# Two matmuls of 256 columns for one of 512 in block 2's first feed-forward layer, and norm sums in halves of 128 columns

## Chip, cores and metric

One core of one Trainium2 chip runs the whole program in one launch. The metric is device time in microseconds (us), the median over several runs; smaller is better.

## What is computed

Two transformer-like blocks for 256 tokens of width 1024. The first has a gated linear attention branch, a spatial gating branch and a retrieval of single-neuron experts. The second takes the tokens `x` and a context `ctx` of 256 rows and begins with the same feed-forward layer for both:

```
def rmsnorm_2(x, w):
    xf = x.astype(jnp.float32)
    y = xf * lax.rsqrt(jnp.mean(xf * xf, axis=-1, keepdims=True) + EPS)
    return (y * w.astype(jnp.float32)).astype(x.dtype)

def swiglu(h, w13, w2):
    a, b = jnp.split(h @ w13, 2, axis=-1)
    return (jax.nn.silu(a) * b) @ w2
...
        x = x + 0.5 * g1x * swiglu(modulate(rmsnorm_2(x, norm_ffn1[l]), sh1x, sc1x), w13_ffn1[l], w2_ffn1[l])
        ctx = ctx + 0.5 * g1c * swiglu(modulate(rmsnorm_2(ctx, norm_ffn1[l]), sh1c, sc1c), w13_ffn1[l], w2_ffn1[l])
```

After it come retention, a Fourier branch, a second feed-forward layer for the tokens alone, and a last norm. The width `D_MODEL` is 1024, `D_FF` is 2816.

## The kernel before

Activations lie with the features on the 128 partitions and the 256 tokens (T) along the free dimension, in 8 chunks (KD). A weight unit is 128 by 1024 floats (512 KB). SyncE loads it into `raw`; ScalarE casts it to `whi` (fp32r, line 112) and VectorE makes the rest `wlo` (line 113). An activation is kept as two parts likewise. A product is three matmuls, `mm3` (lines 248 to 251): whi with the high part, whi with the low part, wlo with the high part. Each matmul has its own weight load (PEld in the profile), of 128 columns.

The order of the work is a hand-made list of items that `Emit.run` (line 91) walks through; each weight unit is an item, and three units are split ahead. Small steps are put behind later units with `em.later`.

`ffn` (line 468) is a feed-forward layer. There are 22 steps j. `up` (line 539) makes the two halves of the first product for step j, two units each of 24 matmuls, and `down` (line 557) adds the second product of step j - 2, one unit of 24 matmuls of 256 columns. In block 2's first layer the steps from `early` = 2 on have tokens and context side by side in the tiles `nxh` and `nxl` (128 by 8 by 512 floats), so that one matmul streams 512 columns into one PSUM bank. Steps 0 and 1 take a copy of the tokens that is not yet normalized, `y` (258 columns), and the context, `nhi` and `nlo` (256 columns), apart. Behind the steps the context's own second product follows (`down_c`, line 1623), in matmuls of 256 columns.

The norms' sums of squares over the features are made on TensorE: `ones_sum` (line 259) multiplies a 128 by 128 matrix of ones with the squares, plain fp32. Eight places call it: `norm1`, `norm2`, `ctx_norm` (twice), `sum_x` in `rest_c` (line 1463; it runs in step 6 of the first layer, between its two halves), `x_sums`, `rest_f2`, and `f2_done` (line 1961), the end of the program. Seven give it one tile of 512 columns, the last gives it four, `qs`, as ScalarE makes them. The trace lists each fp32 matmul as two.

`rest_c` also has a sum of its own, line 1450: eight fp32 matmuls of 256 columns, ahead of the context's product of step 1.

`GAP` (line 39) is a table of paddings in floats, put ahead of tiles; `open_d` puts GAP["nx"] ahead of `nxh`.

Of the kernel before, what the change touches and what calls it, by code (L numbers as in the profile page):

```python
# [20 lines left out]
P = 128  # L21
T = 256
# [13 lines left out]

TS = 320

GAP = {"n": 48, "ya": 40, "y": 48, "mc": 0, "nx": 32, "q": 48, "v": 16, "sc": 48, "y01": 0, "fo": 40, "f2": 32, "mh": 48}

NE = 7

# [160 lines left out]
def body(ctx, tc, I, out):  # L203
    nc = tc.nc
    act, dve, pe, pool = nc.scalar, nc.vector, nc.tensor, nc.gpsimd
# [10 lines left out]
    def bankA():  # L216
        return psA.tile([P, 512], F32, name="acc", tag="acc")

    def bankB():
        return psB.tile([P, 512], F32, name="wk", tag="wk")  # L220
# [27 lines left out]
    def mm3(o, whi, wlo, xhi, xlo, start, stop):  # L248
        pe.matmul(o, whi, xhi, start=start, stop=False)  # L249
        pe.matmul(o, whi, xlo, start=False, stop=False)  # L250
        pe.matmul(o, wlo, xhi, start=False, stop=stop)  # L251
# [6 lines left out]

    def ones_sum(qs, bank=bankB):
        ps = bank()  # L260
        for j, q in enumerate(qs):
            for a in range(2):
                pe.matmul(ps[:, :T], ones, q[:, a * T:a * T + T], start=j + a == 0, stop=a == 1 and j == len(qs) - 1)
        return ps

    def qsum(qs):
# [102 lines left out]
    def gap(pl, name):  # L369
        if GAP[name]:  # L370
            pl.tile([P, GAP[name]], F32, name="gap" + name, tag="gap" + name)

# [8 lines left out]
    def apair():  # L381
        return [npool.tile([P, T], F32R, name=n, tag=n, bufs=2) for n in ("ah", "al")]

    def split(src, hi, lo):
        act.copy(hi, src)  # L385
        dve.tensor_tensor(out=lo, in0=src, in1=hi, op=ALU.subtract)  # L386
# [6 lines left out]
    def chunks(o, hi, lo, x, width, order=range(KD)):  # L393

        xh, xl = x
        for k in order:
            sl = slice(k * P, k * P + P)
            mm3(o, hi[:, sl], lo[:, sl], xh[:, k, :width], xl[:, k, :width], k == order[0], k == order[-1])
# [54 lines left out]
    def gate_y(pa_, pb_, wk):  # L453

        ca, cb = shifted(pa_, wk), shifted(pb_, wk)
        s = wk.tile([P, T], F32, name="xs", tag="xs", bufs=2)
        u = wk.tile([P, T], F32, name="nn", tag="nn", bufs=3)
        dve.tensor_tensor(out=s, in0=pa_[:, :T], in1=E_["r"], op=ALU.mult)
        dve.tensor_tensor(out=u, in0=pb_[:, :T], in1=E_["r"], op=ALU.mult)

        def silu():
            act.activation(out=s, in_=s, func=AF.Silu, bias=ca)

        def prod():
            dve.scalar_tensor_tensor(out=s, in0=u, scalar=cb[:, 0:1], in1=s, op0=ALU.add, op1=ALU.mult)
        return s, silu, prod

    def ffn(w13, w2, y, nx, wk, done, rest, early, ctx=None, mc=None):

        acc = Acc()
        hold = {}
        items = []

        def gate_c(j):
            ps = hold.pop(("c", j))
            s = wk().tile([P, T], F32, name="cs", tag="cs", bufs=1)
            act.activation(out=s, in_=ps[:, 0:T], func=AF.Silu)  # L480
            dve.tensor_tensor(out=s, in0=s, in1=ps[:, T:], op=ALU.mult)
            em.later(lambda: split(s, *mc(j)))

        def gate(j):
            pa_, pb_ = hold.pop(("ps", j, 0)), hold.pop(("ps", j, 1))
            both = ctx is not None and j >= early
            if j < early:
                s, silu, prod = gate_y(pa_, pb_, wk())
            else:
                w = 2 * T if both else T  # L490
                f = wk().tile([P, w], F32, name="s2", tag="s2", bufs=2)
                s = f[:, :T]

                def silu():
                    act.activation(out=f, in_=pa_[:, :w], func=AF.Silu)

                def prod():
                    dve.tensor_tensor(out=f, in0=f, in1=pb_[:, :w], op=ALU.mult)

            def low():  # L500
                hold["m", j] = apair()
                split(s, *hold["m", j])
                if both:
                    split(f[:, T:], *mc(j))

            if j < 2:
                silu()
                if ctx is not None:
                    prod()
                else:  # L510
                    em.later(prod, 1)
                em.later(low, 0 if ctx is not None else 1)
                return

            hold["low", j] = low
            if ctx is not None or j == NFF - 1:
                silu()
                prod()
            else:
                em.later(silu)  # L520
                em.later(prod, 1)

        def bank(j, half):
            if ctx is None:
                return bankA() if j == 2 else bankB()
            return bankA() if j == half == 1 else bankB()

        def up0(sp):
            if ctx is not None:
                c = hold["c", 0] = bankB()  # L530
                for n, (hi, lo) in enumerate(sp):
                    chunks(c[:, n * T:n * T + T], hi, lo, ctx(), T)
            ps = [bank(0, n) for n in range(2)]
            hold["ps", 0, 0], hold["ps", 0, 1] = ps
            mm3s([p[:, :T + 2] for p in ps], sp, *y(), T + 2)
            if ctx is not None:
                em.later(lambda: gate_c(0))

        def up(j, half):
            def fn(hi, lo):  # L540
                ps = hold["ps", j, half] = bank(j, half)
                if j >= early:
                    w = T if ctx is None else 2 * T
                    chunks(ps[:, :w], hi, lo, nx(), w)
                else:
                    if ctx is not None:
                        if half == 1:
                            hold["c", j] = bankA()
                        chunks(hold["c", j][:, half * T:half * T + T], hi, lo, ctx(), T)
                    chunks(ps[:, :T + 2], hi, lo, y(), T + 2)  # L550
                if half == 0:
                    if j < early and ctx is not None:
                        em.later(lambda: gate_c(j))
                    em.later(lambda: gate(j))
            return fn

        def down(j):
            def fn(hi, lo):
                mh, ml = hold.pop(("m", j))
                acc.step(hi, lo, mh, ml, j == 0, j == NFF - 1)  # L560
                f = hold.pop(("low", j + 2), None)
                if f is not None and ctx is None and j + 2 == NFF - 1:
                    em.soon.append(f)
                elif f is not None:
                    em.later(f, 0 if ctx is not None else 1)
                if j == NFF - 1:
                    done(acc)
            return fn

        def begun():  # L570
            rest()
            em.later(lambda: gate(0), 0 if ctx is not None else 1)

        items += [("w", [w13[0], w13[NFF]], up0), ("e", None, begun)]
        for j in range(1, NFF):
            items.append(("w", w13[NFF + j], up(j, 1)))
            items.append(("w", w13[j], up(j, 0)))
            if ctx is not None and j > 1:
                items.append(("w", w2[j - 2], down(j - 2)))
            elif 2 < j < NFF - 1:  # L580
                for n in (0, 1) if j == 3 else (j - 2,):
                    items.append(("w", w2[n], down(n)))

        for n in range(NFF - 2 if ctx is not None else NFF - 3, NFF):
            items.append(("w", w2[n], down(n)))
        return items
# [10 lines left out]
    ones = const.tile([P, P], F32, name="ones")  # L597
# [102 lines left out]
    ya = (pa.tile([P, 4, T], F32R, name="yah"), pa.tile([P, 4, T], F32R, name="yal"))  # L700
# [247 lines left out]
    mh = pa.tile([P, KD, T], F32R, name="mh")  # L948
# [357 lines left out]
    sc = 0  # L1306
    for j in range(NQ, 16):
        n = min(j - 1, sc + (3 if j > NQ else 0))
        items += [score(i) for i in range(sc, n)]
        sc = n  # L1310
# [188 lines left out]
    n = len(ADA_A)  # L1499
# [82 lines left out]
    def mc(j):  # L1582

        t, c = (B["n"], j - 2) if j in MCN else (M["mc"], j if j < 2 else j - KD)
        return [m[:, c, :] for m in t]
# [418 lines left out]
    for h in range(4):  # L2004
        g = [gunit(h, j) for j in range(4)]
        v = tm(I["wv"][4 * h:4 * h + 4], [XN, XC], ev_v, bankA)
        k, q = qk(h, 1), qk(h, 0)
# [116 lines left out]
```

## Time and profile before

| what | value |
| --- | --- |
| median of 3 runs | 1959.22 us (1956.07 to 1961.68) |
| the profiled execution's own time | 1956.7 us |
| its span | 1955.0 us |
| TensorE busy, matmuls | 1938.9 us (99%) |
| TensorE busy, weight loads | 1860.3 us (95%) |
| VectorE busy | 1391.5 us (71%) |
| ScalarE busy | 1018.0 us (52%) |

A matmul's record lasts longer than the distance to the next one, since they overlap: 277 ns for 256 columns, with the next start some 113 to 118 ns later. So the cost of a matmul is read from starts, or from how many fall into a stretch, and not from its duration. The granted clock in the page's slices is full throughout.

### The profile page before, as it was taken

How to read it: one execution, taken by the hardware profiler on the slowest of the kernel's cores; microseconds unless marked ns; L12 is line 12 of the kernel's file. 1: busy time of each engine (PE TensorE's matmuls, PEld its weight loads, DVE VectorE, ACT ScalarE, POOL GpSimd, SP SyncE). 2: the span in 40 equal slices, each digit the busy share in tenths (PEclk: the TensorE clock that was granted, in tenths of full speed). 3: DMA queues.
4: the chain of work that ended last, by engine and by line, in shares of the span. 5: the costliest groups of instructions: out<-in, count | busy, mean ns of one | idle time of the engine just before them, and what ended most of it. 6: DMA issues, size and time to landing. Idle time of an engine off the chain costs nothing.

```text
span 1955.0 us, 37794 instructions
## 1 busy us (share of the span) xinstructions
PE 1938.9 (99%) x15348; PEld 1860.3 (95%) x15348; DVE 1391.5 (71%) x2282; ACT 1018.0 (52%) x1510; POOL 152.8 (8%) x296
## 2 busy tenths in 40 slices
PE   9999999999999999999999999999999999999998
PEld 8899999999999999999988888899989999999998
DVE  7667788987776776798866776578754556578655
ACT  6554655467776555555563333245744455446444
POOL 0000011111112001111000000010000000000000
PEclk9999999999999999999999999999999999999999
DMA  7655577766667778897755566677643334455663
GB/s 245 199 165 186 184 227 231 253 219 198 202 202 238 251 243 271 289 295 254 216 198 171 185 198 217 199 243 268 203 124 97 116 110 133 149 176 172 195 195 128
DMA packets 110094, 393.18 MB, mean 201 GB/s; under 512 B 14103, under 2 KB 14487, under 8 KB 109536
## 3 DMA queue, kind: packets, MB, share of 16 engines
q1 hardware_dynamic: 85968, 310.55, 50.5%
q0 software_dynamic: 22944, 77.52, 12.0%
q8 instruction: 120, 1.97, 0.4%
q10 hardware_dynamic: 1008, 2.70, 0.4%
q14 instruction: 54, 0.44, 0.1%
HBM read 371.84 MB, written 18.87 MB: 200 GB/s over the span
## 4 chain that ended last, share of the span: by engine, by line
PE 93%; DMA 2%; DVE 2%; ACT 1%; issue 0%; SPq 0%; ACTq 0%; DVEq 0%; POOLq 0%
PE wk L249 18%; PE wk L251 17%; PE wk L250 17%; PE acc L250 10%; PE acc L249 10%; PE acc L251 10%; PE acc L425 2%; PE acc L427 2%; PE acc L426 2%; DVE wlo L113 1%; PE acc L1255 1%; PE acc L1256 1%; DMA raw<-w_dram 1%; DMA raw<-f2a_dram 1%; ACT whi L112 1%; DMA raw<-f13a_dram 1%
## 5 line engine op out<-in xcount | busy, mean ns | idle before, releaser
L113 DVE TENSOR_TENSOR wlo<-raw,whi 128x1024 fp32r<-128x1024 f32 x587 | 716.4, 1223 | 464.2 <-ACT whi L112 460.5
L112 ACT CAST whi<-raw 128x1024 fp32r<-128x1024 f32 x587 | 615.9, 1050 | 650.9 <-PE wk L250 276.4
L249 PE MATMUL wk<-nhi,whi 128*128 128x256 f32 x1648 | 465.1, 282 | 1.3 <-ACT whi L112 1.3
L251 PE MATMUL wk<-nhi,wlo 128*128 128x256 f32 x1648 | 457.1, 277 | 0.8 <-DVE wlo L113 0.8
L250 PE MATMUL wk<-nlo,whi 128*128 128x256 f32 x1648 | 457.2, 277 | 0.0
L250 PE MATMUL acc<-al,whi 128*128 128x256 f32 x1376 | 382.9, 278 | 0.1
L249 PE MATMUL acc<-ah,whi 128*128 128x256 f32 x1376 | 382.6, 278 | 0.0
L251 PE MATMUL acc<-ah,wlo 128*128 128x256 f32 x1376 | 382.4, 278 | 0.0
L249 PEld LDWEIGHTS wk<-nhi,whi 128*128 128x128 f32 x1648 | 309.9, 188 | 2.4 <-ACT whi L112 1.5
L251 PEld LDWEIGHTS wk<-nhi,wlo 128*128 128x128 f32 x1648 | 310.0, 188 | 1.0 <-DVE wlo L113 1.0
L250 PEld LDWEIGHTS wk<-nlo,whi 128*128 128x128 f32 x1648 | 310.2, 188 | 0.5 <-issue 0.5
L250 PEld LDWEIGHTS acc<-al,whi 128*128 128x128 f32 x1376 | 259.4, 189 | 1.4 <-DVE al L386 0.5
L249 PEld LDWEIGHTS acc<-ah,whi 128*128 128x128 f32 x1376 | 258.5, 188 | 0.8
L251 PEld LDWEIGHTS acc<-ah,wlo 128*128 128x128 f32 x1376 | 259.2, 188 | 0.0
L249 PE MATMUL wk<-nxh,whi 128*128 128x512 f32 (+1 forms) x544 | 188.4, 346 | 0.0
L251 PE MATMUL wk<-nxh,wlo 128*128 128x512 f32 (+1 forms) x544 | 187.5, 345 | 0.0
L250 PE MATMUL wk<-nxl,whi 128*128 128x512 f32 (+1 forms) x544 | 186.5, 343 | 0.0
L385 ACT CAST ah<-early 128x256 fp32r<-128x256 f32 x128 | 52.1, 407 | 150.3 <-PE acc L251 147.0
L251 PEld LDWEIGHTS wk<-nxh,wlo 128*128 128x128 f32 x544 | 102.1, 188 | 14.1
L250 PEld LDWEIGHTS wk<-nxl,whi 128*128 128x128 f32 x544 | 102.2, 188 | 12.4
L249 PEld LDWEIGHTS wk<-nxh,whi 128*128 128x128 f32 x544 | 102.4, 188 | 11.5
L1269 POOL DMA_DIRECT2D uD<-act x128 | 69.1, 540 | 367.6 <-ACT act L1268 308.0
(526 smaller groups left out, 3345.2 us busy)
## 6 DMA issues: line engine op xcount, KB each, us to landing
raw<-pu_dram SPq DMA_DIRECT2D x128, 512.0 KB, 4.0
raw<-pv_dram SPq DMA_DIRECT2D x128, 512.0 KB, 4.4
row<-ada_dram POOLq DMA_DIRECT2D x59, 512.0 KB, 4.6
raw<-f13a_dram SPq DMA_DIRECT2D x44, 512.0 KB, 3.5
raw<-f2a_dram SPq DMA_DIRECT2D x44, 512.0 KB, 4.5
raw<-f13b_dram SPq DMA_DIRECT2D x44, 512.0 KB, 3.5
raw<-w_dram SPq DMA_DIRECT2D x41, 512.0 KB, 4.3
uD<-act POOLq DMA_DIRECT2D x128, 128.0 KB, 4.0
```

The costliest lines, as they stand in the source:

```text
L112: nc.scalar.copy(hi, r)
L113: nc.vector.tensor_tensor(out=lo, in0=r, in1=hi, op=ALU.subtract)
L249: pe.matmul(o, whi, xhi, start=start, stop=False)
L250: pe.matmul(o, whi, xlo, start=False, stop=False)
L251: pe.matmul(o, wlo, xhi, start=False, stop=stop)
L385: act.copy(hi, src)
L425: pe.matmul(o, xh[:, k, ts], hi[:, sl], start=k == 0, stop=False)
L426: pe.matmul(o, xh[:, k, ts], lo[:, sl], start=False, stop=False)
L427: pe.matmul(o, xl[:, k, ts], hi[:, sl], start=False, stop=k == KD - 1)
L1255: pe.matmul(o, p2[:, k, :, t], ph[:, k, :, t], start=True, stop=False)
L1256: pe.matmul(o, p2[:, k, :, t], p1[:, k, :, t], start=False, stop=True)
L1269: pool.dma_start(out=uD[:, b, :], in_=u)
```

## The change

`up` of block 2's first layer makes one product over the 256 token columns and then one over the 256 context columns, with the same weights, in the two halves of the same PSUM bank. `ones_sum` makes the first 128 columns of its sum over all its inputs, and then the other 128. GAP["nx"] becomes 0, which moves `nxh`, `nxl` and the tiles behind them in their pool by 128 bytes a partition.

```
-GAP = {"n": 48, "ya": 40, "y": 48, "mc": 0, "nx": 32, "q": 48, "v": 16, "sc": 48, "y01": 0, "fo": 40, "f2": 32, "mh": 48}
+GAP = {"n": 48, "ya": 40, "y": 48, "mc": 0, "nx": 0, "q": 48, "v": 16, "sc": 48, "y01": 0, "fo": 40, "f2": 32, "mh": 48}
...
     def ones_sum(qs, bank=bankB):
         ps = bank()
-        for j, q in enumerate(qs):
-            for a in range(2):
-                pe.matmul(ps[:, :T], ones, q[:, a * T:a * T + T], start=j + a == 0, stop=a == 1 and j == len(qs) - 1)
+        for c in range(0, T, P):
+            for j, q in enumerate(qs):
+                for a in range(0, 2 * T, T):
+                    pe.matmul(ps[:, c:c + P], ones, q[:, a + c:a + c + P], start=j + a == 0,
+                              stop=a == T and j == len(qs) - 1)
         return ps
...
                 if j >= early:
-                    w = T if ctx is None else 2 * T
-                    chunks(ps[:, :w], hi, lo, nx(), w)
+                    for c in range(1 if ctx is None else 2):
+                        ts = slice(c * T, c * T + T)
+                        chunks(ps[:, ts], hi, lo, [m[:, :, ts] for m in nx()], T)
```

TensorE's order where `sum_x` stands between two units of the first layer; the names are out<-moving,weights with buffer numbers, `wk` is a PSUM bank, `scr` holds the squares. Before:

```order
L250 MATMUL wk_13926<-nxl_13081,whi_13842 128x512
L251 MATMUL wk_13926<-nxh_13080,wlo_13843 128x512
L263 MATMUL wk_13957<-scr_13185,ones_98 128x256 x2
L249 MATMUL wk_13966<-nxh_13080,whi_13877 128x512
L250 MATMUL wk_13966<-nxl_13081,whi_13877 128x512
```

and now, at the same place:

```order
L250 MATMUL wk_14123<-nxl_13086,whi_14015 128x256
L251 MATMUL wk_14123<-nxh_13085,wlo_14016 128x256
L264 MATMUL wk_14178<-scr_13190,ones_98 128x128 x4
L249 MATMUL wk_14189<-nxh_13085,whi_14074 128x256
L250 MATMUL wk_14189<-nxl_13086,whi_14074 128x256
```

The sum stands between the same two units; the matmuls on both sides are 48 to a unit instead of 24.

TensorE's last rows, in `f2_done`, where the four `scr` are the four tiles of squares in the order in which ScalarE makes them. Before:

```order
L251 MATMUL acc_21173<-ah_23068,wlo_23038 128x256
L263 MATMUL wk_23140<-scr_23125,ones_98 128x256 x2
L263 MATMUL wk_23140<-scr_23129,ones_98 128x256 x2
L263 MATMUL wk_23140<-scr_23133,ones_98 128x256 x2
L263 MATMUL wk_23140<-scr_23137,ones_98 128x256 x2
```

and now:

```order
L251 MATMUL acc_22146<-ah_24041,wlo_24011 128x256
L264 MATMUL wk_24113<-scr_24098,ones_98 128x128 x2
L264 MATMUL wk_24113<-scr_24102,ones_98 128x128 x2
L264 MATMUL wk_24113<-scr_24106,ones_98 128x128 x2
L264 MATMUL wk_24113<-scr_24110,ones_98 128x128 x2
L264 MATMUL wk_24113<-scr_24098,ones_98 128x128 x2
L264 MATMUL wk_24113<-scr_24102,ones_98 128x128 x2
L264 MATMUL wk_24113<-scr_24106,ones_98 128x128 x2
L264 MATMUL wk_24113<-scr_24110,ones_98 128x128 x2
```

The second half's matmuls of the first three tiles now stand behind those of the fourth tile's first half.

## Rows read from the trace of the kernel before

**Rows 1.** The page, its first part: busy us, share of the span, instructions.

```profile
PE 1938.9 (99%) x15348; PEld 1860.3 (95%) x15348; DVE 1391.5 (71%) x2282; ACT 1018.0 (52%) x1510; POOL 152.8 (8%) x296
```

**Rows 2.** Group of line 249 (250 and 251 have one alike): busy us, mean ns | idle.

```profile
L249 PE MATMUL wk<-nxh,whi 128*128 128x512 f32 x320 | 126.4, 395 | 0.0
```

**Rows 3.** Who waited for whom, TensorE, longest first.

```profile
PE wk L249 <- ACT whi L112: 1.3, 1, 1.3
```

**Rows 4.** Timeline, TensorE, one step of the first layer: start, us.

```profile
1123.25 0.40 PE L249 MATMUL wk<-nxh,whi 128*128 128x512 f32 x1
...
1134.25 0.28 PE L249 MATMUL acc<-ah,whi 128*128 128x256 f32 x1
```

**Rows 5.** Timeline, TensorE, from the steps' end to `x_sums` and behind it.

```profile
1286.34 0.28 PE L249 MATMUL acc<-ah,whi 128*128 128x256 f32 x1
...
1308.95 1.03 PE L263 MATMUL acc<-scr,ones 128*128 128x256 f32 x4
...
1309.93 0.28 PE L250 MATMUL wk<-nlo,whi 128*128 128x256 f32 x1
```

**Rows 6.** Windows, busy us (instructions) of PE, PEld, DVE, ACT, POOL; clock, DMA share.

```profile
1100.00:1120.00 20.00, 20.00 (x101) 16.92 (x100) 14.42 (x22) 5.31 (x7) 2.05 (x4) 1.00 0.66 204
640.00:780.00 140.00, 140.00 (x1238) 140.00 (x1237) 98.36 (x129) 69.64 (x103) 16.06 (x30) 1.00 0.79 253
1289.00:1306.00 17.00, 17.00 (x146) 17.00 (x146) 15.09 (x27) 10.39 (x14) 1.58 (x3) 1.00 0.73 245
1312.00:1348.00 36.00, 36.00 (x320) 36.00 (x319) 32.09 (x46) 15.76 (x20) 4.23 (x8) 1.00 0.92 326
875.00:910.00 35.00, 35.00 (x299) 35.00 (x298) 32.87 (x50) 17.65 (x26) 4.28 (x8) 1.00 0.82 269
```

**Rows 7.** Timeline, TensorE, behind line 1450's sum.

```profile
996.86 3.62 PE L1450 MATMUL acc<-scr,x 128*128 128x256 f32 x16
...
1000.43 0.28 PE L250 MATMUL acc<-nlo,whi 128*128 128x256 f32 x1
...
1001.49 0.28 PE L250 MATMUL acc<-nlo,whi 128*128 128x256 f32 x1
```

**Rows 8.** Timeline, TensorE, the scores of block 1: fp32 matmuls of 128 columns.

```profile
227.81 0.61 PE L1092 MATMUL acc<-k,q 128*128 128x128 f32 x4
228.25 1.06 PE L1092 MATMUL acc<-k,scr 128*128 128x128 f32 x8
229.06 0.37 PE L249 MATMUL wk<-nhi,whi 128*128 128x256 f32 x1
229.26 0.28 PE L250 MATMUL wk<-nlo,whi 128*128 128x256 f32 x1
...
231.77 0.28 PE L251 MATMUL wk<-nhi,wlo 128*128 128x256 f32 x1
```

**Rows 9.** Timeline and window, `norm1`'s sum and the units behind it.

```profile
17.91 1.13 PE L263 MATMUL acc<-scr,ones 128*128 128x256 f32 x4
...
20.00:35.00 15.00, 15.00 (x129) 15.00 (x129) 14.43 (x25) 8.09 (x13) 0.00 (x0) 1.00 0.93 287
```

**Rows 10.** Timeline, `sum_x`, and when `nxl` is written and first used.

```profile
1008.99 3.25 DVE L337 SCALAR_TENSOR_TENSOR nxl<-x,modx,nxh 128x256 fp32r<-128x256 f32 x8
1011.77 0.39 PE L249 MATMUL wk<-nxh,whi 128*128 128x512 f32 x1
1072.59 1.03 PE L263 MATMUL wk<-scr,ones 128*128 128x256 f32 x4
```

**Rows 11.** Timeline, the end of the program.

```profile
1942.60 1.41 ACT L1969 ACTIVATE scr<-x 128x512 f32<-128x512 f32 x2
1942.75 3.61 PE L263 MATMUL wk<-scr,ones 128*128 128x256 f32 x16
1944.17 0.63 ACT L1969 ACTIVATE scr<-x 128x512 f32<-128x512 f32 x1 [0.15 <-DVE x L1526]
1946.40 0.47 ACT L1971 ACTIVATE rr<-wk,eps 128x256 f32<-128x256 f32 x1 [1.60 <-PE wk L263]
```

## The prediction

> **What bounds the kernel now.** I read the page's first part before anything else: TensorE's matmuls fill 99% of the span and VectorE only 71% [rows 1]. Then the list of waits: TensorE's longest single wait of the whole program is 1.3 us [rows 3]. So the time is the sum of the matmuls' spacings, and what the change is worth is a question of spacing, since a matmul's record overlaps the next one. For that I read the timeline and the windows.
>
> In the layer that is changed, a step has 48 matmuls of 512 columns in 1134.25 - 1123.25 = 11.00 us, 229.2 ns each [rows 4]. The 256-column matmuls do not have one spacing but two. From 1286.34 to 1308.95 there are 192 of them (8 units of 24): 117.8 ns each [rows 5]. A window counts some 2.4 instructions too many (those that only reach into it); without them 640:780 has 113.3 ns and 1312:1348 113.4, but 1289:1306 and 875:910 have 118 [rows 6]. I call them the **fast** pace, 113.3 ns, and the **slow** pace, 117.8. The clock is 1.00 and the weight loads are busy without a gap in all four windows, so neither explains it. Nor do the tiles: the context's `nhi` and `nlo` are read slowly up to 1308.95 and fast behind it, at the same places. What stands between is the fp32 sum of `x_sums` [rows 5]. A pace holds for tens of microseconds and is drawn anew where something breaks the row of matmuls. All down units of the first layer run slowly now, behind their 512-column units.
>
> **The price of a split.** Two matmuls of 256 for one of 512 cost 2 x 117.8 - 229.2 = +6.4 ns at the slow pace and 2 x 113.3 - 229.2 = -2.6 ns at the fast one. There are 3 x 320 = 960 of them [rows 2], so the term lies between +6.1 and -2.5 us, and the pace decides its sign. The 960 added weight loads are in these spacings, as both were read where each matmul has its load.
>
> The Trainium skill (TensorE: Matmul & The Clock Gate, Back-to-back issue gap) speaks against the split: it gives a gap of N / 2.4 + 2.5 ns for N columns, so a fixed part is paid twice, 2 x 109.2 - 215.8 = +2.5 ns, an estimate from that page of +2.4 us for the 960. The trace has none of these gaps: 229.2 ns, and two spacings for 256. With the page's figure in place of my split terms below (+1.4 and -1.9) the sum would be about +0.7 instead of -2.2 us.
>
> **Which pace, where.** The fp32 sum of line 1450 is unchanged, and behind it `nhi` runs slowly: 9 matmuls in 1001.49 - 1000.43 = 1.06 us, 117.8 ns each [rows 7]. I take that pace to hold, through 258-column units, into the new 256-column units at 1011.77 [rows 10]. The next break is `sum_x` at 1072.59 [rows 10], which is now eight passes of 128 columns. The nearest rows are the scores of block 1, fp32 of 128 columns with a 256-column unit behind: 0.20 us to the unit's second matmul, then 22 spacings in 231.77 - 229.26 = 2.51 us, 114 ns each, the first few included [rows 8]. The timeline has the same behind the six other places of line 1092. Behind 256-column sums the pace came out either way: fast behind `x_sums`, slow behind `norm1` and line 1450 [rows 5, 7, 9]. So: slow up to `sum_x`, fast from there on. The terms:
>
> - Steps 2 to 5 and half of step 6: 4 x 48 + 24 = 216 splits at +6.4 ns: +1.4 us.
> - The other 744 splits at -2.6 ns: -1.9 us.
> - 16 down units behind `sum_x`, 384 matmuls from slow to fast at -4.5 ns: -1.7 us.
> - Behind the steps, 192 - 24 = 168 matmuls up to `x_sums` [rows 5], likewise: -0.8 us.
> - Seven single sums. Now 1308.95 to 1309.93 = 0.98 us with the step to the second matmul [rows 5]. By the scores, 12 passes take 1.25 us, that is 111.5 ns a pass with a last one of 31, and then 0.20 [rows 8]; eight give 7 x 0.1115 + 0.031 + 0.20 = 1.01. +0.03 each, +0.2 us. The latency up to the root grows by as little, and no TensorE wait hangs on it [rows 3].
> - The last sum, which nothing hides. Now its passes go tile by tile, 3.61 us from 1942.75, and the fourth tile's square is ready at 1944.80, before its turn [rows 11]. In the new order the first half wants the fourth tile sooner than it is there: passes 13 to 16 start about 1944.86 and end at 1945.31, and only then come the 16 of the second half, 16 x 111.5 ns, to 1947.1, with a last latency to about 1947.3. The root now starts at 1946.40 [rows 11], the reciprocal, the products and the output behind it: +0.9 us.
> - Behind `norm1` the units are slow now ((129 - 2.4) / 15 us is 118 ns) for some 15 us [rows 9]. A fast pace there would be 132 x 4.5 ns = -0.6 us, but VectorE is busy 14.43 of 15 us and may hold it; half of it, -0.3 us.
>
> Sum: 1.4 - 1.9 - 1.7 - 0.8 + 0.2 + 0.9 - 0.3 = **-2.2 us**. Against the profiled execution that is 1956.7 - 2.2 = 1954.5 us. The median of the runs shown lies 2.5 us above it, and I put the difference on the median: 1959.2 - 2.2 = **1957.0 us**.
>
> Costed at nothing: the gates read a full bank as before, behind the second half. `nxl` is complete at 1008.99 + 3.25 = 1012.24 [rows 10]; the token half now wants its last chunk 21 matmuls behind 1011.77, at 1014.2 instead of 1016.6, so 2 us of cover are left; without it the wait would be a part of VectorE's 0.4 us for a chunk. The splits of the weights keep their distance, as a unit lasts as long as before within 3%. The move by 128 bytes: since one tile has both paces at one place, I take 0; its bounds are those of the split, as it could decide the pace.
>
> **The rivals.**
> *All fast.* The pace turns fast already at 1011.77. The 512-column units that preceded each slow down unit are gone; against it, line 1450's sum leaves a slow pace today. The 216 splits give -0.6 instead of +1.4, and four more down units -0.4: sum -4.6, 1954.6 us.
> *Slow throughout, a fixed part in every matmul.* If 117.8 ns is what this layer's 256-column matmuls cost, with its row loads and VectorE work beside them, no sum mends it: 960 x 6.4 = +6.1, +1.1 from the sums: 1966.4 us. For it: every down unit of the layer, also those behind today's `sum_x`, and the weight loads, busy 16.92 of 20 us there now [rows 6], get no slack any more. Against it: the same code at 1312:1348 is fast with VectorE busy 32 of 36 us. A step gains 0.23 us when fast and loses 0.31 when slow, and the other terms then cancel (+1.1 - 0.8 - 0.3), so the change is a loss from nine slow steps of the twenty on. This is the skill's rule above with the rows' price.
> *The split costs nothing either way.* The two halves take the time of the whole, as 229.2 lies between 226.6 and 235.6; the down units stay slow. Then only the sums' +1.1 is left: 1960.3 us.
>
> **How the numbers follow.** Slow then fast 0.42, all fast 0.28, slow 0.20, nothing 0.10. The range takes in the first, second and fourth with a spread of some 3 us, since the pace also changes where nothing is edited (875:910, 35 us at the slow pace, would be 1.4 us faster [rows 6]) and the three runs spread over 5.6 us; of the slow case it holds the part in which only some steps are slow: 1952 to 1964 us. A change of 0.3% is 5.9 us, about what a measurement can tell here. Faster than 1953.3: a third of *all fast* and a quarter of the forecast, 0.2. Slower than 1965.1: three quarters of *slow*, 0.15. Within: 0.65.
>
> **What would show it.** Right: no 512-column matmul in `up`, about 170 TensorE instructions in 20 us around 1050, about 179 around 1150 to 1270; the eight passes of `sum_x` in some 0.8 us and 113 ns spacing behind them; the last root about 0.9 us further from its sum's first pass. Wrong: 118 ns behind `sum_x`, or slow stretches opening elsewhere in place of these; a TensorE wait on `nxl` at the first unit; an end no later than before.

## The result, and the profile after

The changed kernel takes 1969.36 us, the median of 8 runs (1965.54 to 1974.76); the kernel before, beside it, 1956.49 us (1951.82 to 1961.68). The ratio is 1.0058, with a 95% interval of 1.0044 to 1.0073: slower by 0.6%, and outside the forecast range. The profiled execution, the fastest of the eight, took 1965.54 us with a span of 1963.8, that is 8.8 us more than the profiled execution of before.

The page of the changed kernel, its first part, answers to [rows 1]:

```profile
PE 1946.6 (99%) x16352; PEld 1906.4 (97%) x16352; DVE 1391.1 (71%) x2282; ACT 1019.6 (52%) x1510; POOL 153.2 (8%) x296
```

TensorE is still what the time is made of, and the other engines do what they did. The windows of the changed kernel, TensorE alone (busy us, instructions, clock, DMA share, GB/s):

```profile
205.00:222.00 17.00, 17.00 (x147) 1.00 0.64 200
930.00:980.00 50.00, 50.00 (x427) 1.00 0.69 211
1380.00:1396.00 16.00, 16.00 (x138) 1.00 0.66 198
...
1015.00:1070.00 55.00, 55.00 (x488) 1.00 0.46 143
1080.00:1300.00 220.00, 220.00 (x1870) 1.00 0.63 197
...
1860.00:1930.00 70.00, 70.00 (x621) 1.00 0.66 194
```

In the kernel before the first three windows, whose matmuls are the same, and the last one read:

```profile
205.00:222.00 17.00, 17.00 (x152) 1.00 0.70 219
930.00:980.00 50.00, 50.00 (x444) 1.00 0.72 223
1380.00:1396.00 16.00, 16.00 (x144) 1.00 0.70 207
...
1860.00:1930.00 70.00, 70.00 (x620) 1.00 0.63 195
```

The granted clock is 1.00 in all of them. Divide the length by the instructions (less the two or so that only reach in): 55 us with 488 is the fast pace, 113 ns, and 220 us with 1870 is the slow one, 117.8 ns. So the layer is **fast ahead of `sum_x` and slow behind it**, the reverse of what was forecast, and three stretches behind other halved sums have gone from fast to slow. The timeline shows it, behind line 1450's sum (now line 1453) and behind `sum_x`, as in [rows 7] and [rows 10]:

```profile
1001.99 0.28 PE L250 MATMUL acc<-nlo,whi 128*128 128x256 f32 x1
...
1003.02 0.28 PE L250 MATMUL acc<-nlo,whi 128*128 128x256 f32 x1
...
1072.98 1.05 PE L264 MATMUL wk<-scr,ones 128*128 128x128 f32 x8
1073.79 0.36 PE L249 MATMUL wk<-nxh,whi 128*128 128x256 f32 x1
1073.99 0.28 PE L250 MATMUL wk<-nxl,whi 128*128 128x256 f32 x1
...
1076.11 0.28 PE L250 MATMUL wk<-nxl,whi 128*128 128x256 f32 x1
```

Nine spacings in 1.03 us behind the first sum are 114 ns each; 18 in 2.12 us behind `sum_x` are 117.8 each, from the second matmul on.

The end of the program answers to [rows 11]:

```profile
1950.74 4.60 PE L264 MATMUL wk<-scr,ones 128*128 128x128 f32 x32
1952.06 0.52 PEld L264 LDWEIGHTS wk<-scr,ones 128*128 128x128 f32 x4 [0.26 <-ACT scr L1972]
1952.84 2.31 PEld L264 LDWEIGHTS wk<-scr,ones 128*128 128x128 f32 x20 [0.26 <-ACT scr L1972]
1955.38 0.47 ACT L1974 ACTIVATE rr<-wk,eps 128x256 f32<-128x256 f32 x1 [2.59 <-PE wk L264]
```

With the starts of three later sums in both kernels, the root's 1955.38 - 1946.40 = 8.98 us can be laid out by place. The changed kernel's sums (`x_sums`, the mixing norm's, and `rest_f2`'s):

```profile
1314.14 1.05 PE L264 MATMUL acc<-scr,ones 128*128 128x128 f32 x8
1374.19 1.05 PE L264 MATMUL wk<-scr,ones 128*128 128x128 f32 x8
1776.20 1.05 PE L264 MATMUL acc<-scr,ones 128*128 128x128 f32 x8
```

and the last two in the kernel before:

```profile
1367.55 1.02 PE L263 MATMUL wk<-scr,ones 128*128 128x256 f32 x4
1768.12 1.03 PE L263 MATMUL acc<-scr,ones 128*128 128x256 f32 x4
```

| from, to | before, us | after, us | difference |
| --- | --- | --- | --- |
| start to `sum_x` | 1072.59 | 1072.98 | +0.4 |
| `sum_x` to `x_sums` | 236.36 | 241.16 | +4.8 |
| `x_sums` to the mixing norm's sum | 58.60 | 60.05 | +1.4 |
| to the sum in `rest_f2` | 400.57 | 402.01 | +1.4 |
| to the last sum's first pass | 174.63 | 174.54 | -0.1 |
| to the root | 3.65 | 4.64 | +1.0 |

The second row is the heart. In it every unit is slow: its 744 splits at +6.4 ns are +4.8 us, and the down units stay as slow as they were. The forecast had -4.4 us there. In the third row the pace is fast in both kernels; there the difference is a few long spacings, the longest of 1.1 us, in which TensorE waited 0.8 us for `wlo`. The fourth and fifth rows hold two stretches that the prediction did not price, the one behind the mixing norm's sum and the 175 us behind the sum in `rest_f2`; the second of them is as fast here as before.

### The profile page after: what moved, and what is told of

Its sections match the earlier page's. It is cut to its first block, busy times and chain, and to the rows that moved or that the text cites. A ratio compares the mean times of both kernels' runs of the same rounds, so it can differ in the third digit from the quotient of the medians.

```text
span 1963.8 us, 39802 instructions
## 1 busy us (share of the span) xinstructions
PE 1946.6 (99%) x16352; PEld 1906.4 (97%) x16352; DVE 1391.1 (71%) x2282; ACT 1019.6 (52%) x1510; POOL 153.2 (8%) x296
## 4 chain that ended last, share of the span: by engine, by line
PE 89%; DVE 4%; DMA 4%; ACT 2%; issue 1%; SPq 0%; DVEq 0%; ACTq 0%; POOLq 0%
PE wk L249 17%; PE wk L251 17%; PE wk L250 17%; PE acc L250 9%; PE acc L251 9%; PE acc L249 9%; PE acc L427 2%; PE acc L429 2%; PE acc L428 2%; DVE wlo L113 2%; DMA raw<-pv_dram 1%; ACT whi L112 1%; DMA raw<-f2a_dram 1%; PE acc L1258 1%; PE acc L1259 1%
## 5 line engine op out<-in xcount | busy, mean ns | idle before, releaser
L249 PE MATMUL wk<-nxh,whi 128*128 128x256 f32 x864 | 241.0, 279 | 0.0
L251 PE MATMUL wk<-nxh,wlo 128*128 128x256 f32 x864 | 240.9, 279 | 0.0
L250 PE MATMUL wk<-nxl,whi 128*128 128x256 f32 x864 | 240.9, 279 | 0.0
L250 PEld LDWEIGHTS wk<-nxl,whi 128*128 128x128 f32 x864 | 164.3, 190 | 0.0
L249 PEld LDWEIGHTS wk<-nxh,whi 128*128 128x128 f32 x864 | 162.2, 188 | 0.0
L251 PEld LDWEIGHTS wk<-nxh,wlo 128*128 128x128 f32 x864 | 162.2, 188 | 0.0
```

## Experiments

Each kernel was timed in turn with the kernel before, whose median moved between 1958.7 and 1961.6 from one set of runs to the next, so the ratios are compared and not the medians alone.

**The parts alone.** First the split with the padding, the sums left 256 columns wide (against the changed kernel):

```
-        for c in range(0, T, P):
-            for j, q in enumerate(qs):
-                for a in range(0, 2 * T, T):
-                    pe.matmul(ps[:, c:c + P], ones, q[:, a + c:a + c + P], start=j + a == 0,
-                              stop=a == T and j == len(qs) - 1)
+        for j, q in enumerate(qs):
+            for a in range(2):
+                pe.matmul(ps[:, :T], ones, q[:, a * T:a * T + T], start=j + a == 0, stop=a == 1 and j == len(qs) - 1)
```

> The split of the first layer and the padding as in the changed kernel, the norms' sums as before, 256 columns wide. Theory (the width of a sum decides the pace behind it: behind the halved sum_x of the changed kernel there are 1870 TensorE instructions in 220 us, 117.8 ns, where the kernel before has the fast pace behind its 256-wide sum in the units that could show it): behind sum_x the pace is now fast, about 1940 instructions in 220 us, 113.3 ns, and behind the first sums as in the kernel before. Time: from line 1450's sum to the last step all is fast, 960 x -2.6 ns = -2.5 us, and some 550 down matmuls at -4.5 ns = -2.5 us, less what sum_x costs itself: 1951 to 1954 us where the kernel before has 1956.5. Rival (the row loads and VectorE's dots beside the units hold the layer at the slow pace, no matter what sum stands ahead): 1870 in 220 us behind sum_x as in the changed kernel, the first 60 us fast; 1959 to 1963 us.

Measured: 1957.27 us, ratio 0.9995 (0.998 to 1.001). The windows of this run:

```profile
930.00:980.00 50.00, 50.00 (x427) 1.00 0.67 217
1015.00:1070.00 55.00, 55.00 (x470) 1.00 0.44 141
1080.00:1300.00 220.00, 220.00 (x1943) 1.00 0.63 205
```

Behind a 256-wide `sum_x` the same units, with the same row loads and VectorE work beside them, are fast. The rival that the layer's surroundings hold it slow falls. The time missed the expected 1951 to 1954: two stretches ahead are slow, 930 to 980 and 1015 to 1070, and the expectation was reckoned from a kernel before of 1956.5 us, which took 1958.9 beside this run.

Then the halved sums alone (the same lines the other way round, against the kernel before), and the changed kernel with only `sum_x` made whole again, by a function `ones_whole` that has the loops of before:

> Only the halved sums; the first layer has its 512-column matmuls and the padding of before. Theory (a halved sum turns the fast pace slow): the stretches behind norm2 (205 to 223), behind the context norm's sum (929 to 990) and behind the context's mixing norm (1373 to 1407) are slow as in the changed kernel, +0.8, +2.3 and +1.3 us, the tail +1.0, seven sums +0.2, the layer's steps as before: 1956.5 + 5.6 = 1962 us, 1960 to 1964. Rival (the pace is drawn afresh in each build whatever the sum, or it hangs on the moved addresses, which this kernel has not): those stretches are as in the kernel before and only the tail and the sums are left, 1957.7 us.

```
-            s1 = ones_sum(qs[:1])
+            s1 = ones_whole(qs[:1])
```

> The changed kernel with one sum undone: sum_x is 256 columns wide again, the seven others stay halved. Theory: from sum_x to x_sums the pace is fast, about 1940 TensorE instructions in 220 us in place of 1870, that is 240.3 us times 4.5 / 117.8 = -9.2 us against the changed kernel, and the halved x_sums behind it may then leave a slow pace for its 60 us, +2.3: between -9 and -6 us, 1960 to 1963 us. Rival (the work beside the layer holds it slow): as the changed kernel, 1969 us, 1870 in 220 us.

Halved sums alone: 1966.21 us, ratio 1.0033 (1.0021 to 1.0045). The windows of this run:

```profile
205.00:222.00 17.00, 17.00 (x152) 1.00 0.58 193
930.00:980.00 50.00, 50.00 (x427) 1.00 0.66 211
1318.00:1345.00 27.00, 27.00 (x231) 1.00 0.93 328
1380.00:1396.00 16.00, 16.00 (x144) 1.00 0.64 200
```

The sums cost by themselves, as the theory said, and more than the expected 1960 to 1964 us, but at only one of the three places that it named, the context norm's: behind `norm2` and the mixing norm it is fast here, and behind `x_sums`, where the changed kernel was fast, it is slow. So "a halved sum turns fast into slow" is too strong. The largest part of what this execution lost against the profiled one of before lies in a stretch that I had not looked at, behind the sum in `rest_f2`. From that sum to the last one it takes 1951.37 - 1771.44 = 179.93 us, where the kernel before and the changed kernel took 174.6 and 174.5. The last window of this run, against 620 in the kernel before, shows it:

```profile
1860.00:1930.00 70.00, 70.00 (x597) 1.00 0.59 185
```

With `sum_x` whole: 1962.7 us, ratio 1.0022 (1.0007 to 1.0037), and

```profile
1080.00:1300.00 220.00, 220.00 (x1940) 1.00 0.63 205
```

So that one sum, eight passes of some 0.8 us, sets the pace of the 240 us behind it: with the seven others still halved, undoing it alone turns the stretch fast.

**Where the ones lie.** The nearest rows of the prediction, the scores of block 1, are fp32 passes of 128 columns too and leave a fast pace. By the built program's addresses their weights start at a multiple of 64 bytes in each partition, the ones of the norms 32 bytes past one. The allocation of the ones can be moved by putting small constants ahead of them, with every other large tile left in place (so the addresses of the built programs show):

```
+    eps = const.tile([P, 1], F32, name="eps")
     ones = const.tile([P, P], F32, name="ones")
...
-    eps = const.tile([P, 1], F32, name="eps")
```

> The changed kernel, but the matrix of ones starts 32 bytes further in each partition (the small constant eps is put ahead of it); all that lies behind both stays where it was. The scores of block 1 are fp32 passes of 128 columns too and leave a fast pace, and their weights start at a multiple of 64 bytes, those of the norms' sums 32 bytes past one. Sub-theory (where the weights of the fp32 sum start decides): fast behind the halved sums, 1940 in 220 us behind sum_x, some -13 us against the changed kernel, 1956 us. Otherwise, if the width or the number of the passes decides: as the changed kernel, 1969 us, 1870 in 220 us.

Measured: 1958.22 us, ratio 0.9999 (0.9984 to 1.0014): 0.6% less than the changed kernel for the place of one tile. The windows:

```profile
930.00:980.00 50.00, 50.00 (x443) 1.00 0.71 223
...
1080.00:1300.00 220.00, 220.00 (x1940) 1.00 0.63 206
```

Not every halved sum followed: behind `x_sums` this trace is slow, where the changed kernel was fast.

With `eps` and `eps2` ahead of the ones (64 bytes further, again 32 past a multiple of 64), and the changed kernel twice more for its trace:

> The changed kernel, but the ones start 64 bytes further (two small constants ahead of them) in place of the 32 bytes of the run with the ones moved, so that they again lie 32 bytes past a multiple of 64; all that lies behind them stays. If the start of the ones within 64 bytes decides: slow behind the halved sums as in the changed kernel, 1870 TensorE instructions in the 220 us behind sum_x, and 1969 us. If any move of the ones would have done, since each build draws its paces anew: fast behind some of the sums, most of all sum_x, 1940 in 220 us, and 1956 to 1961 us.

> The changed kernel once more, for its trace: is the pace behind each sum the same in another execution? If the build fixes it: slow behind norm1, norm2, the context norm's sum, sum_x (1870 TensorE instructions in 1080 to 1300) and the mixing norm's sum, fast behind line 1450's and x_sums, 1965 to 1970 us. If each execution draws it: another pattern, and where sum_x leaves a fast pace some 9 us less, 1957 to 1961 us.

> The changed kernel a third time, for its trace, with the same two outcomes: the same pattern as in the first (1870 TensorE instructions in 1080 to 1300) if the build fixes the pace behind sum_x, another one if the execution draws it.

Moved by 64 bytes: 1972.38 us, ratio 1.0067 (1.0049 to 1.0085). The changed kernel again: 1976.88 and 1972.51 us, with these windows in the first and the second:

```profile
1015.00:1070.00 55.00, 55.00 (x469) 1.00 0.41 133
1080.00:1300.00 220.00, 220.00 (x1870) 1.00 0.60 196
...
1860.00:1930.00 70.00, 70.00 (x596) 1.00 0.60 185
```

```profile
1015.00:1070.00 55.00, 55.00 (x469) 1.00 0.40 126
1080.00:1300.00 220.00, 220.00 (x1871) 1.00 0.61 198
```

`sum_x` left the slow pace in all three traces of the changed kernel, while line 1450's sum left the fast one in the first and the slow one in the other two. The slower of the two is also slow behind the sum in `rest_f2` (179.92 us from there to the last sum). So a pace is drawn anew by each execution, at odds that differ by place. The kernel with 64 bytes points the same way: its profiled execution, of 1959.75 us, was fast behind `sum_x`, and its six others took 1968.6 to 1975.3. Two further traces:

> The changed kernel with the ones 64 bytes further, once more, for its trace. Its first trace was fast behind sum_x (1942 TensorE instructions in 1080 to 1300) in an execution of 1959.75 us, while its six other executions took 1968.6 to 1975.3. If a pace is drawn by each execution and those were the slow draws: about 1972 us, and 1870 in that stretch.

> The changed kernel with the ones 32 bytes further, once more, for its trace: its twelve executions took 1954.0 to 1966.4 us. If that place of the ones leaves the fast pace behind sum_x each time: 1940 TensorE instructions in 1080 to 1300 and 1954 to 1962 us. If that too is drawn by each execution: 1870 possible, with some 9 us more.

They took 1969.59 us (64 bytes) and 1952.26 us (32 bytes), with, in this order:

```profile
1080.00:1300.00 220.00, 220.00 (x1870) 1.00 0.62 197
```

```profile
1080.00:1300.00 220.00, 220.00 (x1939) 1.00 0.64 208
```

Last a second multiple of 64 (`eps`, `eps2` and `lg` ahead of the ones, 96 bytes further), and the opposite case, wide sums with the ones 32 bytes further:

> The changed kernel with the ones 96 bytes further (three small constants ahead of them), so that they start at a multiple of 64 bytes again, but at another one than in the run with 32. So far behind the halved sum_x: ones at their old place slow in 3 of 3 traces and 10 executions of 1965 to 1977 us; 64 bytes further fast once and slow once, with 7 of 8 executions over 1968; 32 bytes further fast in 2 of 2 and 13 executions of 1952 to 1966. If a multiple of 64 makes the fast pace likely: 1940 TensorE instructions in 1080 to 1300 and a median of 1955 to 1961 us. If the run with 32 was a place by itself: 1870 there, and 1967 to 1973 us.

> The split and the padding of the changed kernel, the sums 256 columns wide as before, and the ones 32 bytes further (a multiple of 64), to see whether the place of the ones also serves wide sums. If it does as with the halved sums: fast behind norm1 too and behind the context norm's sum, which were slow in the run with the split and the sums of before (16 us and 60 us at 4 per cent, -0.6 and -2.3 us): 1957.3 - 2.9 = 1954.4 us. If the place of the ones matters for passes of 128 columns alone: 1957.3 us, the same stretches slow.

96 bytes: 1959.72 us, ratio 0.9988 (0.997 to 1.0006). Wide sums with 32 bytes: 1967.14 us, ratio 1.0037 (1.0021 to 1.0053), against 0.9995 for wide sums with the ones at their old place; I had expected the wide sums to gain or to stay, and they lost. Their windows, in this order:

```profile
1080.00:1300.00 220.00, 220.00 (x1940) 1.00 0.63 205
```

```profile
1080.00:1300.00 220.00, 220.00 (x1870) 1.00 0.62 196
```

All traces with split units behind `sum_x` and the padding taken away, but for the version at the end of this section:

| `sum_x` | ones moved by | pace behind it in the traces | executions, us |
| --- | --- | --- | --- |
| halved | 0 (the change) | slow, slow, slow | 10, 1965.5 to 1976.9 |
| halved | 64 bytes | fast, slow | 8: one 1959.8, seven 1968.6 to 1975.3 |
| halved | 32 bytes | fast, fast | 13, 1952.3 to 1966.4 |
| halved | 96 bytes | fast | 12, 1953.0 to 1963.4 |
| wide | 0 | fast | 12, 1953.9 to 1969.0 |
| wide, others halved | 0 | fast | 12, 1960.3 to 1973.3 |
| wide | 32 bytes | slow | 12, 1958.7 to 1974.0 |

Behind `sum_x`, passes of 128 columns and of 256 did best with the ones at different places. It is a matter of odds: in the traces of kernels with halved sums, the pace behind a halved sum ahead of 1400 us (six places) was slow 20 times of 28 with the ones at their old place, and 7 of 24 at a multiple of 64 bytes (the version below counted in). The difference sits at three of the six places, the context norm's sum, `sum_x` and the mixing norm's (12 of 13 against 2 of 12); at `norm1`, `norm2` and `x_sums` it is 8 of 15 against 5 of 12, which tells nothing. With the ones 64 bytes further the two traces were slow 4 times of 12. That is no worse than at a multiple of 64, though this start lies 32 bytes past one, like the old place; only its time is like the changed kernel's. So that a multiple of 64 is what counts is not shown: four starts were tried, and two of them did well.

The seventh stretch, the 175 us behind the sum in `rest_f2`, shows no link with the ones or the width. In the sixteen traces of this case it took 174.5 to 174.6 us eight times and 179.9 eight times: with halved sums twice slow of five at the old place, twice of four at a multiple of 64 and twice of two at 64 bytes, with wide sums twice of five. A trace's time holds this draw of 5.3 us too.

**The padding.** The split alone, with the padding of before (against the kernel before):

```
-                    w = T if ctx is None else 2 * T
-                    chunks(ps[:, :w], hi, lo, nx(), w)
+                    for c in range(1 if ctx is None else 2):
+                        ts = slice(c * T, c * T + T)
+                        chunks(ps[:, ts], hi, lo, [m[:, :, ts] for m in nx()], T)
```

> The split alone, the sums 256 columns wide and the padding of 32 floats ahead of nxh kept. If the move by 128 bytes does nothing: as the run with the split and the move, 1957.3 us, 1943 TensorE instructions in the 220 us behind sum_x, 470 in the 55 us ahead of it (slow behind line 1450's sum). If the move decides the pace in the layer: 1870 in the 220 us, some 9 us more, 1966 us.

And the kernel before without its padding:

```
-GAP = {... "mc": 0, "nx": 32, "q": 48, ...}
+GAP = {... "mc": 0, "nx": 0, "q": 48, ...}
```

> The kernel before with the padding ahead of nxh taken away and nothing else: no split, no halved sum. In the run with the split and the padding kept, each unit on nxh ran at 117.8 ns and each down unit right behind it at 113.5, so the place of the moving tile decides the pace within one row of matmuls, against some phase that the row holds. If that also rules the 512-column units, the 16 down units behind them change from slow to fast (384 + 168 matmuls up to x_sums at -4.5 ns = -2.5 us; 512-column matmuls as before): 1956.4 us where the kernel before has 1958.9, and 1289 to 1306 has 153 TensorE instructions in place of 146. If the 512-column matmuls themselves leave the slow pace behind them, wherever they lie: no change, 1958.9 us, 146.

The split with the padding kept: 1965.85 us, ratio 1.0036 (1.0024 to 1.0048), where the split without it had 0.9995. Its windows ahead of `sum_x` and behind it, and TensorE's timeline behind it at the first matmuls of a down unit, of the two units of `up` that follow, and of the next down unit:

```profile
1015.00:1070.00 55.00, 55.00 (x469) 1.00 0.45 143
1080.00:1300.00 220.00, 220.00 (x1885) 1.00 0.61 198
```

```profile
1107.69 0.28 PE L249 MATMUL acc<-ah,whi 128*128 128x256 f32 x1
...
1110.42 0.28 PE L249 MATMUL wk<-nxh,whi 128*128 128x256 f32 x1
...
1121.72 0.28 PE L249 MATMUL acc<-ah,whi 128*128 128x256 f32 x1
```

The down unit's 24 matmuls take 2.73 us, 113.8 ns each; the 96 of `up` behind them 11.30 us, 117.7 each; and so on in each step up to `x_sums`, without anything between them that breaks the row. So the pace is not a property of the row alone: within one row it changes with the tile that is streamed. Nor is it one of the tile's place alone: ahead of `sum_x` in this trace, with the tiles at the same places, both kinds of units are slow (469 in 55 us). In this program `nxh` starts 160 bytes past a multiple of 256, `ah` and all other 256-wide tiles 32 past one, as `nxh` does without the padding. Costed at nothing in the prediction, the 128 bytes decide here whether `up` is fast behind a `sum_x` that leaves the down units fast. Of the 8.9 us between the profiled executions of the split with the padding and without it, (1311.98 - 1073.22) - (1305.94 - 1073.75) = 6.6 lie between `sum_x` and `x_sums`; another 5.3 are the draw behind `rest_f2`, and other stretches give some back.

The kernel before without its padding: 1962.76 us, ratio 1.0013 (0.9998 to 1.0027). The same rows:

```profile
1111.74 0.39 PE L249 MATMUL wk<-nxh,whi 128*128 128x512 f32 x1
...
1122.94 0.28 PE L249 MATMUL acc<-ah,whi 128*128 128x256 f32 x1
...
1125.66 0.39 PE L249 MATMUL wk<-nxh,whi 128*128 128x512 f32 x1
```

In this trace the 512-column matmuls take 11.20 / 48 = 233.3 ns instead of 229.2 [rows 4], and the down units 2.72 / 24 = 113.3 instead of 117.8. The 512s have two paces too, and in these traces the padding goes with their faster one and with slow down units. I had expected the downs to gain and the 512s to stay. The two effects nearly cancel, and the time of the whole cannot be told from that of the kernel before.

**A version of both.** The change, the ones 32 bytes further, and the last sum tile by tile as before:

```
-        act.activation(out=r, in_=ones_sum(qs)[:, :T], ...)
+        act.activation(out=r, in_=ones_whole(qs)[:, :T], ...)
```

> The changed kernel with the ones 32 bytes further and the last sum of the program in the order of before (tile by tile, 256 columns), which no fp32r matmul follows. The tail: from the first pass to the root 3.65 us again in place of 4.64, so 1.0 us less than the run with the ones moved: 1957.2 us, and 1940 TensorE instructions in 1080 to 1300. If the draws of the paces are wider than this: anything from 1953 to 1961 us.

Measured: 1957.15 us, ratio 0.9986 (0.9967 to 1.0005). Its tail:

```profile
1949.85 3.62 PE L272 MATMUL wk<-scr,ones 128*128 128x256 f32 x16
...
1953.51 0.47 ACT L1981 ACTIVATE rr<-wk,eps 128x256 f32<-128x256 f32 x1 [1.68 <-PE wk L272]
```

3.66 us from the first pass to the root, so the 1.0 us is had back. Its executions spread from 1950.4 to 1964.9 us; the profiled one, 1963.67 us, was fast behind `sum_x` but slow behind four of the other five sums ahead of 1400 us and behind the one in `rest_f2`. That the median is the expected 1957.2 is in part luck, with draws this wide. The version cannot be told from the kernel before.

## Why the prediction was wrong, step by step

- **What bounds the kernel: right.** TensorE stayed at 99%, the time is the sum of spacings, no wait on `nxl` appeared, and the clock took no part.
- **The two paces and the price of a split: right in size.** All fast the split gives 113.3 ns in 220 us, all slow 117.8 [rows 5, 6]. The rival priced for *slow throughout* gave 1966.4 us and came nearest to the median of 1969.36, but by its number alone: its mechanism (a fixed part in every matmul, or the layer's surroundings) is refuted by the split alone, which is fast behind `sum_x`. The estimate from the Trainium skill (TensorE: Matmul & The Clock Gate, Back-to-back issue gap), +2.5 ns a split, was met by neither pace: +6.4 or -2.6. That section of the Trainium skill calls its formula the gap of an isolated matmul, which the prediction left out; the roofline that it gives for a stream of weight loads and matmuls, some 131 ns at 512 columns, does not agree with this trace's 229.2 either.
- **"From `sum_x` on fast": the step that failed.** I took the pace from the scores [rows 8] because they are fp32 passes of 128 columns, overlooked that their weights lie elsewhere, and took the pace behind them for that of any halved sum. The forecast's three terms behind `sum_x` come to -4.4 us; the trace has +4.8, which is 9.2 of the 11.0 us by which the forecast of -2.2 missed the profiled execution's +8.8. The pace behind the halved `sum_x` is slow in three traces of three with the ones where they are, fast in four of four with them at a multiple of 64 bytes, and once fast, once slow at 64 bytes. It is no rule for a halved sum: behind `x_sums`, with the same ones and the same passes, all three traces of the changed kernel are fast. Why the place counts behind one sum and not behind the other stays open.
- **"Slow up to `sum_x`": a likely draw taken as fixed.** Behind line 1450's sum the first trace of the change was fast, its two further ones slow; in all traces with split units it is slow 10 times of 13.
- **The other halved sums: left out.** I had costed seven of them at their passes and `norm1` at half a gain; behind `norm2`, the context's norm and the mixing norm the pace turned slow in the profiled execution. The draw of 5.3 us behind the sum in `rest_f2` was left out too; it fell fast in this execution and slow in one of the two further traces.
- **The passes and the tail: right.** `sum_x` took 1073.99 - 1072.98 = 1.01 us to the second matmul, forecast 1.01. The tail cost 0.99 us, forecast 0.9, with the waits for the third and fourth square in its trace; putting the order back took it away.
- **The move by 128 bytes at nothing: wrong.** I argued that one tile has both paces at one place. That is so, but in the split with the padding kept, behind `sum_x`, it is the place that parts the fast tile from the slow one in one row. The ratios of the two splits differ by 0.0041, some 8 us; 6.6 of them are seen where the padding acts.
- **The range** rested on the paces being independent of the sums' form. With one sum setting 240 us, the slow case needed more than 0.2, and with other sums drawing too, the range a wider upper end.

## What to carry to other kernels

When an engine is full and its instructions have two spacings, a short interruption can set the spacing for hundreds of microseconds behind it: price an edit to the interruption by the work behind it, not by its own length. Take a nearest row only if its operands lie alike, not only its shape, and look at several executions before a pace is called fixed. Then lay out the difference between two traces over the whole program: a stretch that was not edited can hold as much of it as the one that was. A padding in a change is not bookkeeping: run it alone.

## What the runs showed that was not expected

- A spacing of 256-column matmuls of 113.3 or 117.8 ns, and of 512-column ones of 229.2 or 233.3, at a granted clock of 1.00 in both. Which of the two it is goes with the last fp32 interruption and with where the streamed tile starts: with 128 bytes of padding, behind one sum, the units on one tile were slow and those on another fast, step after step in one row.
- The odds of the pace behind a sum of some 0.8 us go with its form together with where its weights start, at some places in the program: 32 or 96 bytes further turned 1969.4 us into 1958.2 and 1959.7; for wide sums 32 bytes did the reverse, 1957.3 to 1967.1.
- Each execution draws anew. Two executions of one program, 1965.5 and 1976.9 us, differ by the stretches that are slow: 5.4 us behind the sum in `rest_f2` (174.5 against 179.9), 3.8 ahead of `sum_x`, the rest in between.

What stays open: what in the row the interruption sets (no view shows it), why the same place gives both paces at times, and why the place counts behind some sums and not behind others. A halved sum differs from a wide one in the width, the number and the total length of its passes at once, and these were not parted. The place of the ones was tried at four starts with halved sums and at two with wide ones. That the weights of the units or the squares have a place to be chosen in the same way was not tried.
